# A list scheduler's prices for TensorE's small fp32 products, in one mixer instead of two

## The chip, the cores and the metric

The kernel runs on one core of a Trainium2 chip. The metric is the device time of one execution in microseconds. A profiled execution is read beside it, with the time of each instruction on TensorE (PE, and PEld for its weight loads), VectorE (DVE), ScalarE (ACT), GpSimd (POOL) and the DMA queues that SyncE (SP) and others issue.

## The reference, cut to what matters

A decoder trunk of two layers on 512 tokens of 1024 channels, in fp32. Each layer is `x <- LN(alpha*x + mixer(x))`, then `x <- LN(alpha*x + hierMoE(x))`. The first layer's mixer is RWKV-7 time mixing with causal pooling, the second's a Conformer convolution with chunkwise retention. The change reaches the second one, here in short:

```python
def conv_retention_mixer(x, w_in, conv_w, conv_b, cln_g, cln_b, gn_g, gn_b, w_out):
    p = x @ w_in
    ca, cb, q, k, v, gr = split(p)                      # 512 channels each
    u = causal_depthwise_conv(ca * sigmoid(cb), conv_w) + conv_b      # width 31
    y_conv = silu(layer_norm(u, cln_g, cln_b))
    ret = head_norm(retention(q, k, v), LN_EPS) * gn_g + gn_b
    y_ret = silu(gr) * ret
    return concatenate([y_conv, y_ret]) @ w_out
```

Retention works on 8 heads of 64 in four chunks of 128 tokens: scores `q k^T` under a decay mask, their product with `v`, a product of `q` with the state of the chunks before, and an update of that state from `k` and `v`. After the mixer the router of the expert stage takes the logits of 36 outputs for each token, from which the top group and its top two of eight experts follow.

## The kernel before, in words

`trunk_kernel` (L2228) runs `mixer0`, `moe`, `mixer1`, `moe` one behind the other. The two mixers are written as streams, Python generators that yield the engine of their next step and the tiles that it needs. `Flow` (L31) is a list scheduler that runs while the program is built: it keeps a clock of its own for every engine (`free`), when each tile is made (`made`) and last used (`used`), and in `run` (L179) it always issues the step that could start first. Where two could start at the same time (within `slack`, 0.05 us in the second mixer), the stream that stands first in the list goes first, except that `dense` goes first while the count of TensorE columns is `short` (L186 to L188). The order in which steps are issued is the order in each engine's queue; on the chip an engine works its queue in that order and waits where an operand is not there. The scheduler's clock comes from `cost` (L64), the price of an instruction by engine, operation and size, and `note` (L89) books it; `clocked` (L141) stretches a price on TensorE where it takes the engine's clock to be low, and counts columns: passes (two for fp32) times output columns times weight rows over 128.

`note` overrides the price of a TensorE product in fp32 with both weight rows and output rows at 64 or fewer: it lands in one quarter of the array, and costs its columns over 2080, or over 1040 where one of the two products before it went to the same quarter; 0.11 us is added where such products begin or end. All this is done in every `Flow`, so in both mixers. A transpose costs 0.107, any other product that is not fp32 its columns over 2330, an fp32 product its columns over 600 and at least 0.21.

The second mixer (L972) issues these streams, in the order of the list at L1440: the first weights' split (`weights`: a high half on ACT, low halves on POOL or DVE), `sums`, `turned`, the router's `ready`, `logits` and `norms` (from `start`, L1462), `join`, `ret_norm` (L1409), `retention` (L1309), `kernels`, `evacuate` (L1222), `conv_norm` (L1270), `taps` (L1145), the other `weights`, `dense` (L1173), `affine` and `turn`. What bears on the prediction:

- `dense` multiplies the input projection in steps of three products (high by high, high by low, low by high), with `x` or the weights `w` as the stationary side; in the trace `pp<-x,wh`, `pp<-x,wl`, `pp<-wh,x` and `pp<-wl,x`. Then it waits for `mc` (the convolution's result, L1190) and takes the first half of the output projection (again `pp<-wh,x`, with 512 columns), and for `mr` (the retention's, L1200) the other half (`pp<-wh,mr`).
- `conv_norm` works after the 124 taps of the convolution on DVE. For each of four blocks of 128 tokens (called the first to the fourth token below): four transposes on TensorE (`pt<-ident,acc`), statistics on DVE (`cst`, `cmv`, `crs`), a power of one column on POOL (`crs`), a scaling on DVE (`cn`), four transposes back (`pt<-ident,cn`), four Silu activations on ACT into `acc`. Then for each of four pieces a copy on ACT and a subtraction on DVE (or POOL, L1304) make the high and low halves `mc` (in the trace `x<-acc` and `x<-acc,x`).
- `retention`, per chunk: transposes of `q` and `k` (`pt<-ident,qkv`; copies `qT`, `kT` on ACT, `qx` on DVE), eight scores (`ps<-qT,kT`), a mask on DVE (`sc`), eight products with `v` (`pr<-qkv,sc`, L1361), from the second chunk on eight with the state (`pr<-R,qx`, L1368), in all but the last eight for the state's update (`ps<-qkv,kz`, L1374), then statistics and scaling on DVE with a power of eight columns on POOL (`rst`, `rmv`, `rrs`, `rn`).
- `ret_norm`: transposes of `rn`, `yr` on ACT, its product with `sgr` on DVE, and the halves `mr`.
- Banks of PSUM are handed out by name, two of each; a request waits until the last but one bank of that name has been given back (`take`, L164).

`moe` (L1562) plans its own order by `run_streams` (L218) and uses none of these prices.

Of the kernel before, what the change touches and what calls it, by code (L numbers as in the profile page):

```python
# [9 lines left out]
F32 = mybir.dt.float32  # L10
# [20 lines left out]
class Flow:  # L31
# [3 lines left out]

    HOP = {"PE": 0.2, "V": 0.13, "A": 0.2, "G": 0.13, "D": 0.0}

    def __init__(self, nc, slack=0.0, lead=1.1):
        self.nc, self.slack, self.lead = nc, slack, lead
        self.free = {e: 0.0 for e in ("PE", "V", "A", "G", "D")}  # L40
        self.made, self.used, self.rings, self.place, self.rooms, self.log = {}, {}, {}, {}, {}, []
        self.version = 0
        self.done = set()
        self.columns, self.warm = {}, {0: False}
        self.quarters = [None, None]
        self.pe, self.V, self.A, self.G, self.D = (
            Flow.Engine(self, n, e) for n, e in (("PE", nc.tensor), ("V", nc.vector), ("A", nc.scalar), ("G", nc.gpsimd),
                                                 ("D", nc.sync)))
# [14 lines left out]
    @staticmethod  # L63
    def cost(e, op, out, ins, alu=None):  # L64
        n = max(math.prod(t.shape[1:]) for t in (out, *ins))
        if e == "D":
            return math.prod(out.shape) * 4 / 355e3
        if e == "PE":
            n = math.prod(out.shape[1:])
            if op == "transpose":  # L70
                return 0.107
            if ins[0].dtype == F32:
                return max(n / 600, 0.21)
            return n / 2330
        scalars = sum(math.prod(t.shape[1:]) == 1 for t in ins) if n > 1 else 0
        if e == "V":
            if op == "reciprocal":
                return 0.066 + 0.0063 * n
            fast = op in ("tensor_scalar", "tensor_copy") and ins[0].space == bass.MemoryType.SB
            return 0.066 + 0.06 * scalars + n / (1700 if fast else 960)  # L80
        if e == "A":
            return (0.24 if len(ins) > 1 else 0.14 if scalars else 0.07) + n / 1170
        if op == "memset":
            return n / 1150
        if alu == OP.pow:
            return 0.3 + 0.165 * n
        return 0.07 + n / (445 if op == "tensor_tensor" else 1050)

    def note(self, e, op, args, kw, r):  # L89
        aps = [v for v in (*args, *kw.values()) if isinstance(v, bass.AP)]  # L90
        out, ins = (kw["out"] if "out" in kw else aps[0]), []
        for v in aps:
            if v is not out:
                ins.append(v)
        t0 = self.free["D" if op == "dma_start" else e]
        for v in ins:
            t0 = max(t0, self.at(v, e))
        k = out.tensor.name
        if k not in self.made:
            n, ring = self.enter(out.tensor)  # L100
            bufs = out.tensor.bufs or out.tensor.tag_meta.bufs
            if n >= bufs:
                t0 = max(t0, self.used.get(ring[n - bufs], 0.0) + 0.1)
        else:
            t0 = max(t0, self.used.get(k, 0.0) if not (e == "PE" and k in self.made) else 0.0)
        d = "D" if op == "dma_start" else e
        c = self.cost(d, op, out, ins, kw.get("op"))
        if e == "PE":

            here = None  # L110
            if op != "transpose" and ins[0].dtype == F32 and ins[0].shape[0] <= 64 and out.shape[0] <= 64:
                here = ins[0].start_partition, out.start_partition
                c = math.prod(out.shape[1:]) / (1040 if here in self.quarters[-2:] else 2080)
            if (here is None) != (self.quarters[-1] is None):
                c += 0.11
            self.quarters = (self.quarters + [here])[-2:]
        t1 = self.clocked(t0, c, out, ins[0], op) if e == "PE" else t0 + c
        self.free[d] = t1
        ready = t1 + (2.0 if d == "D" else 0.0)
        self.made[k] = (ready, d)  # L120
        self.used[k] = max(self.used.get(k, 0.0), ready)
        for v in ins:
            k = v.tensor.name
            self.used[k] = max(self.used.get(k, 0.0), t1)
        self.log.append((e, op, t0, t1, r, getattr(self, 'cur', '-')))
# [133 lines left out]
class Kernel:  # L259
# [39 lines left out]
    def mixer0(self):  # L299
# [2 lines left out]


        nc, tc, a = self.nc, self.tc, self.a
        flow = self.flow = Flow(nc, 0.0, 1.0)
        V, G, A, PE = flow.V, flow.G, flow.A, flow.pe
        mm = PE.matmul
        H2 = (0, 64)
# [1 line left out]
        with ctx:  # L310
# [91 lines left out]
            for t in range(NT):  # L402
                for g in range(2):
                    ps = (pp if g else pi).tile([128, 4, 128], F32, name="pp" if g else "pi")
                    for k in range(4):
                        c = 128 * (4 * g + k)
# [1852 lines left out]
```

## Time and profile before

| | us |
|---|---|
| median of three runs | 908.71 (908.58 to 909.77) |
| profiled execution, its own time | 905.55 |
| its span, first to last instruction | 903.7 |
| busy in the span: PE | 829.2 (92%) |
| PEld | 610.5 (68%) |
| DVE | 616.0 (68%) |
| ACT | 335.3 (37%) |
| POOL | 287.1 (32%) |

The page gives the busy share of every engine and TensorE's granted clock in 40 slices of the span; a view by stretch gives the same for any stretch that one names. In a timeline row, consecutive instructions of one kind are merged: start, time, engine, line, operation, tiles, count, and in brackets the idle time of the engine just before, with what ended it. Every step issued by a stream of a mixer has the line of the helper, L58, so rows are told apart by their tiles. An fp32 product is two instructions (x2) in the trace. Matmuls are pipelined, so merged rows on PE can overlap.

### The profile page before, as it was taken

What the parts mean: (1) busy time and instruction counts of PE and PEld (TensorE: products, weight loads), DVE (VectorE), ACT (ScalarE), POOL (GpSimd) and SP (SyncE); (2) the same over time, 40 slices, a digit from 0 to 9 for tenths busy, and PEclk for the clock granted to TensorE, in tenths of its full rate; (3) what the DMA queues carried; (4) which work ended last, traced back from release to release, by engine and by line L of the source; (5) the groups of instructions that cost most, each with busy time, mean ns of one, the idle gap of its engine ahead of it and who ended that gap; (6) DMA issues with size and microseconds to landing.
All of it is one profiled execution on the core that took longest, in us unless ns stands there. A gap on an engine that the chain in (4) does not pass through costs nothing. (4 is left out here: it accounts for less than half of the span.)

```text
span 903.7 us, 18556 instructions
## 1 busy us (share of the span) xinstructions
PE 829.2 (92%) x7386; PEld 610.5 (68%) x7386; DVE 616.0 (68%) x1450; ACT 335.3 (37%) x672; POOL 287.1 (32%) x302
## 2 busy tenths in 40 slices
PE   7999999899999889999968999999899787999992
PEld 5777666676777655665548889997678664546542
DVE  3586987879587776654576899985554576546457
ACT  4544243433322544444354222224313443333323
POOL 2130332334510335010048965446132018000004
PEclk9999999999999899999989999999799989999997
DMA  7210110101228699898561322323135179878932
GB/s 248 93 49 26 49 49 2 49 25 49 72 63 337 203 372 405 346 416 364 203 184 48 94 94 94 94 94 118 63 141 220 71 265 371 299 285 315 421 165 94
DMA packets 43594, 156.96 MB, mean 174 GB/s; under 512 B 4865, under 2 KB 21377, under 8 KB 35312
## 3 DMA queue, kind: packets, MB, share of 16 engines
q1 hardware_dynamic: 38128, 141.79, 41.5%
q0 software_dynamic: 4224, 9.74, 3.4%
q10 hardware_dynamic: 1152, 4.19, 1.1%
q8 instruction: 60, 0.98, 0.5%
q14 instruction: 30, 0.25, 0.1%
HBM read 154.66 MB, written 6.29 MB: 178 GB/s over the span
## 5 line engine op out<-in xcount | busy, mean ns | idle before, releaser
L58 PE MATMUL pp<-x,wh 128*128 128x512 f32 x480 | 156.9, 408 | 1.3 <-ACT wh L58 1.3
L58 PE MATMUL pp<-wh,x 128*128 128x256 f32 (+1 forms) x544 | 129.8, 326 | 3.5 <-DVE rot L58 2.8
L58 ACT CAST wh<-wr 128x512 fp32r<-128x512 f32 (+1 forms) x82 | 61.4, 776 | 146.1 <-PE pp L58 102.8
L1921 DVE SCALAR_TENSOR_TENSOR x<-x,pcm 128x512 f32<-128x512 f32 x104 | 70.7, 685 | 47.2 <-PE pcm L1919 44.6
L58 PEld LDWEIGHTS pp<-wh,x 128*128 128x128 f32 x544 | 92.8, 195 | 13.8 <-DVE x L58 3.3
L1885 PE MATMUL ph<-we,xt 128*64 128x256 f32 (+2 forms) x928 | 101.8, 383 | 0.0
L58 PEld LDWEIGHTS pp<-x,wh 128*128 128x128 f32 x480 | 84.0, 188 | 24.0 <-issue 7.0
L58 PE MATMUL pp<-x,wl 128*128 128x512 f32 x240 | 94.2, 392 | 0.5 <-DVE wl L58 0.5
L1919 PE MATMUL pcm<-yh,P 128*128 128x512 f32 x200 | 86.0, 430 | 2.7 <-DVEq L2104 1.3
L58 PE MATMUL pp<-wl,x 128*128 128x256 f32 (+1 forms) x272 | 87.0, 320 | 0.0
L1875 ACT ACTIVATE xt<-pt,x 128x128 f32<-128x128 f32 x208 | 78.7, 472 | 20.7 <-PE pt L1869 20.7
L1885 PEld LDWEIGHTS ph<-we,xt 128*64 128x64 f32 (+2 forms) x928 | 58.8, 126 | 37.0 <-issue 10.8
L58 DVE SCALAR_TENSOR_TENSOR ps<-u,cw,ps 128x512 f32<-128x512 f32 x116 | 79.5, 745 | 0.7
L1919 PE MATMUL pcm<-yl,P 128*128 128x512 f32 x200 | 79.3, 396 | 0.0
L58 POOL TENSOR_TENSOR wl<-wr,wh 128x1024 fp32r<-128x1024 f32 x28 | 67.3, 2416 | 27.1 <-ACT wh L58 27.1
L58 DVE SCALAR_TENSOR_TENSOR x<-x,pp 128x512 f32<-128x512 f32 x64 | 43.4, 684 | 34.1 <-PE pp L58 33.9
L1787 POOL DMA_INDIRECT xg<-xd,imx x20 | 19.8, 992 | 141.1 <-PE pt L1869 131.2
L1919 PEld LDWEIGHTS pcm<-yh,P 128*128 128x128 f32 x200 | 37.9, 189 | 25.9 <-DVE P L1911 9.0
L1904 PE MATMUL py<-we,hT 128*64 128x512 f32 (+2 forms) x232 | 52.4, 603 | 2.5 <-ACT hT L1895 2.5
L58 PEld LDWEIGHTS pp<-wl,x 128*128 128x128 f32 x272 | 53.0, 195 | 2.4
L58 PEld LDWEIGHTS pp<-x,wl 128*128 128x128 f32 x240 | 45.1, 188 | 10.8 <-DVE wl L58 0.9
L296 DVE TENSOR_TENSOR yl<-py,yh 128x512 fp32r<-128x512 f32 x50 | 34.4, 690 | 24.1 <-ACT yh L295 24.0
(437 smaller groups left out, 1547.6 us busy)
## 6 DMA issues: line engine op xcount, KB each, us to landing
we<-in_c_experts_dram SPq DMA_DIRECT2D x56, 1536.0 KB, 10.3
wr<-in_c_in_dram SPq DMA_DIRECT2D x18, 512.0 KB, 3.6
x<-in_c_experts_dram SPq DMA_DIRECT2D x8, 1024.0 KB, 11.3
wr<-in_od_w_in_dram SPq DMA_DIRECT2D x7, 1024.0 KB, 5.1
wr<-in_ev_w_out_dram SPq DMA_DIRECT2D x8, 512.0 KB, 3.7
x<-in_c_experts_dram SPq DMA_DIRECT2D x8, 512.0 KB, 9.3
xd<-x ACTq DMA_DIRECT2D x8, 512.0 KB, 3.9
wr<-in_od_w_in_dram SPq DMA_DIRECT2D x8, 512.0 KB, 5.8
```

The lines of the kernel that those rows point to most:

```text
L58: r = f(*args, **kw)
L296: (eng or nc.vector).tensor_tensor(lo, src, hi.bitcast(F32), op=OP.subtract)
L1787: G.indirect_dma_start(out=xg[n % NG], out_offset=None, in_=xd, in_offset=bass.IndirectOffsetOnAxis(ap=idx, axis=0), bounds_check=S - 1, o ...
L1875: A.activation(xt[:, kk], ps[:, k], AF.Identity, scale=gc[:, kk:kk + 1], bias=bc[:, kk:kk + 1])
L1885: mm(hp[r], xt[:, k, r], w[0][:, k], start=k == 0, stop=k == KT - 1)
L1904: mm(ps[r], hT[:, r], w[1][:, h], start=True, stop=True)
L1919: mm(ps, P[:, 128 * t:128 * t + 128], y[:, 512 * half:512 * half + 512], start=n == 0, stop=n == len(ops) - 1)
L1921: V.scalar_tensor_tensor(xs, xs, scale, ps, op0=OP.mult, op1=OP.add, accum_out=total)
```

## The change

`Flow` gets a flag, `quarters`, off unless it is given. `mixer0` gives it, `mixer1` does not. With the flag `note` prices TensorE's products as before. Without it `cost` alone does, and there an fp32 product with both sides at 64 rows or fewer costs 0.027 us and its columns over 1200, at least 0.08; any other fp32 product its columns over 600, at least 0.137 instead of 0.21.

```diff
--- before.py
+++ after.py
@@ -35,14 +35,14 @@
 
     HOP = {"PE": 0.2, "V": 0.13, "A": 0.2, "G": 0.13, "D": 0.0}
 
-    def __init__(self, nc, slack=0.0, lead=1.1):
+    def __init__(self, nc, slack=0.0, lead=1.1, quarters=False):
         self.nc, self.slack, self.lead = nc, slack, lead
+        self.quarters = [None, None] if quarters else None
         self.free = {e: 0.0 for e in ("PE", "V", "A", "G", "D")}
         self.made, self.used, self.rings, self.place, self.rooms, self.log = {}, {}, {}, {}, {}, []
         self.version = 0
         self.done = set()
         self.columns, self.warm = {}, {0: False}
-        self.quarters = [None, None]
         self.pe, self.V, self.A, self.G, self.D = (
             Flow.Engine(self, n, e) for n, e in (("PE", nc.tensor), ("V", nc.vector), ("A", nc.scalar), ("G", nc.gpsimd),
                                                  ("D", nc.sync)))
@@ -70,7 +70,8 @@
             if op == "transpose":
                 return 0.107
             if ins[0].dtype == F32:
-                return max(n / 600, 0.21)
+                narrow = ins[0].shape[0] <= 64 and out.shape[0] <= 64
+                return max(0.027 + n / 1200, 0.08) if narrow else max(n / 600, 0.137)
             return n / 2330
         scalars = sum(math.prod(t.shape[1:]) == 1 for t in ins) if n > 1 else 0
         if e == "V":
@@ -105,12 +106,14 @@
             t0 = max(t0, self.used.get(k, 0.0) if not (e == "PE" and k in self.made) else 0.0)
         d = "D" if op == "dma_start" else e
         c = self.cost(d, op, out, ins, kw.get("op"))
-        if e == "PE":
-
-            here = None
-            if op != "transpose" and ins[0].dtype == F32 and ins[0].shape[0] <= 64 and out.shape[0] <= 64:
-                here = ins[0].start_partition, out.start_partition
-                c = math.prod(out.shape[1:]) / (1040 if here in self.quarters[-2:] else 2080)
+        if e == "PE" and self.quarters:
+
+            here, n = None, math.prod(out.shape[1:])
+            if op != "transpose" and ins[0].dtype == F32:
+                c = max(n / 600, 0.21)
+                if ins[0].shape[0] <= 64 and out.shape[0] <= 64:
+                    here = ins[0].start_partition, out.start_partition
+                    c = n / (1040 if here in self.quarters[-2:] else 2080)
             if (here is None) != (self.quarters[-1] is None):
                 c += 0.11
             self.quarters = (self.quarters + [here])[-2:]
@@ -302,7 +305,7 @@
 
 
         nc, tc, a = self.nc, self.tc, self.a
-        flow = self.flow = Flow(nc, 0.0, 1.0)
+        flow = self.flow = Flow(nc, 0.0, 1.0, quarters=True)
         V, G, A, PE = flow.V, flow.G, flow.A, flow.pe
         mm = PE.matmul
         H2 = (0, 64)
```

## Rows read from the trace of the kernel before

**Rows 1.** Busy time by stretch: from us to us, length, then each engine, granted clock, DMA.

```profile
642.10:712.00 69.90, 68.75 (x396) 57.16 (x396) 32.48 (x92) 17.19 (x27) 15.99 (x13) 0.93 0.33 133
```

**Rows 2.** The same view: the stretch before the output products, and the one after it.

```profile
629.30:642.10 12.80, 6.98 (x49) 6.00 (x48) 7.58 (x11) 10.73 (x23) 5.34 (x3) 0.85 0.42 155
...
642.10:649.10 7.00, 7.00 (x43) 5.04 (x42) 0.81 (x2) 0.17 (x1) 0.00 (x0) 0.55 0.02 7
```

**Rows 3.** Groups by form, TensorE, 600 to 720 us: count | busy us, mean ns | idle before.

```profile
L58 PE MATMUL pr<-qkv,sc 128*128 128x64 f32 x64 | 9.4, 310 | 3.8 <-DVE sc L58 3.8
...
L58 PE MATMUL ps<-x,x 128*128 128x36 f32 x64 | 7.6, 272 | 0.0
...
L58 PE MATMUL pr<-R,qx 64*128 64x64 f32 x48 | 4.2, 327 | 0.0
...
L58 PE MATMUL ps<-qkv,kz 128*64 128x64 f32 x48 | 2.1, 228 | 0.0
```

**Rows 4.** Timeline, TensorE: the first product whose price changes.

```profile
604.06 1.89 PE L58 MATMUL pr<-qkv,sc 128*128 128x64 f32 x16
```

**Rows 5.** Timeline, TensorE: between the third token's two sets of transposes.

```profile
617.32 0.60 PE L58 MATMUL pt<-ident,acc 128*128 128x128 f32 x4
...
617.76 1.90 PE L58 MATMUL pr<-qkv,sc 128*128 128x64 f32 x16
...
620.33 1.11 PE L58 MATMUL pr<-R,qx 64*128 64x64 f32 x16
...
621.37 0.73 PE L58 MATMUL pp<-x,wh 128*128 128x512 f32 x2
...
622.26 0.69 PE L58 MATMUL ps<-qkv,kz 128*64 128x64 f32 x16
...
623.68 0.60 PE L58 MATMUL pt<-ident,cn 128*128 128x128 f32 x4
```

**Rows 6.** Timeline, DVE: conv_norm, qx, yr, the last subtraction, and rn beside POOL.

```profile
619.79 0.81 DVE L58 TENSOR_SCALAR cn<-pt,cmv,crs 128x512 f32<-128x512 f32 x1 [0.73 <-POOL crs L58]
...
630.72 0.69 DVE L58 TENSOR_TENSOR qx<-pt,xz 128x512 f32<-128x512 f32 x1 [0.93 <-ACT qT L58]
...
635.96 1.53 DVE L58 TENSOR_TENSOR yr<-yr,sgr 128x512 f32<-128x512 f32 x1 [1.66 <-ACT yr L58]
...
641.53 0.68 DVE L58 TENSOR_TENSOR x<-acc,x 128x512 fp32r<-128x512 f32 x1
...
665.64 2.88 DVE L58 TENSOR_TENSOR rn<-rn,rrs 128x512 f32<-128x512 f32 x1 [0.57 <-POOL rrs L58]
```

**Rows 7.** Timeline, ACT: the weight cast, the fourth Silu, the first yr.

```profile
629.15 1.05 ACT L58 CAST wh<-wr 128x1024 fp32r<-128x1024 f32 x1 [3.33 <-POOL crs L58]
...
631.07 1.51 ACT L58 ACTIVATE acc<-pt,vec 128x128 f32<-128x128 f32 x4
...
634.37 1.56 ACT L58 ACTIVATE yr<-pt,vec 128x128 f32<-128x128 f32 x4
```

**Rows 8.** Timeline, TensorE: the third chunk and the first output product.

```profile
638.74 3.67 PE L58 MATMUL pr<-qkv,sc 128*128 128x64 f32 x16 [3.78 <-DVE sc L58]
...
642.18 0.77 PE L58 MATMUL pp<-wh,x 128*128 128x512 f32 x1
...
643.74 1.97 PE L58 MATMUL pr<-R,qx 64*128 64x64 f32 x16
...
648.50 0.68 PE L58 MATMUL ps<-qkv,kz 128*64 128x64 f32 x16
```

**Rows 9.** Timeline, POOL: the second token's power, and low halves of weights.

```profile
611.71 0.93 POOL L58 TENSOR_TENSOR crs<-crs,nhalf 128x1 f32<-128x1 f32 x1 [1.14 <-DVE crs L58]
...
612.61 2.39 POOL L58 TENSOR_TENSOR wl<-wr,wh 128x1024 fp32r<-128x1024 f32 x1
...
634.59 2.35 POOL L58 TENSOR_TENSOR wl<-wr,wh 128x1024 fp32r<-128x1024 f32 x1 [1.97 <-ACT wh L58]
...
665.58 5.20 POOL L58 TENSOR_TENSOR wl<-wr,wh 128x1024 fp32r<-128x1024 f32 x2
```

## The prediction, made before the change was run

> **What bounds the kernel now.** I read the stretches first. From 642.10 to 712.00 us, the rest of the second mixer, TensorE is busy 68.75 of 69.90 us [rows 1]: there the time is TensorE's work, whatever its order. From 712.00 on the second expert stage runs; it has a planner of its own that the diff does not touch, so what the mixer gains or loses is handed on to the end. The exception is the stretch just ahead: from 629.30 to 642.10 TensorE is busy 6.98 of 12.80 us, and in the 7.00 us after it the granted clock averages 0.55, that is nearly all at 1.2 and not 2.4 GHz [rows 2]. Call this the hole. The dense products of the input projection have run out there, and those of the output projection wait for all four pieces of `mc`, the result of `conv_norm`. So the chain of `conv_norm`, four tokens one behind the other (the Silu writes the `acc` tiles that the next token's transposes read), sets when the hole ends, and TensorE's work outside it sets the rest.
>
> **What changes.** In the first mixer nothing: its flow sets `quarters`, and the branch in `note` then gives every F32 product the price it has now. In the second mixer no product has both sides at 64 rows or fewer (scores write 128 rows, the `kz` products have 128-row weights), so the two-quarter prices never held there. What is left is the floor of a wide F32 product, 0.21 before and 0.137 after; it bites below 126 columns. That is 128 products: 32 `pr<-qkv,sc`, 24 `pr<-R,qx`, 24 `ps<-qkv,kz`, 32 of the router and 16 of its constants; each is two instructions in the trace, hence x64, x48, x48 and x64 [rows 3]. Scores keep 128/600 = 0.213. No instruction is added, removed or changed, no DMA either (SP's loads follow the steps that free their buffers); only the order written into each engine's queue can move, and only behind the first product with a new price. That is the `pr` batch at 604.06 [rows 4]: all before it keeps its order, and so its cost is nothing.
>
> **How the prices stand to the chip.** In the third token's stretch eight `pr` take 1.90 us, eight `R,qx` 1.11, eight `kz` 0.69 [rows 5], together 3.70. The scheduler now books 24 x 0.21 = 5.04, afterwards 24 x 0.137 = 3.29. The new sum is nearer (0.41 short against 1.34 over), though `pr` alone is then booked at 1.10 for 1.90.
>
> **Term A, the third token.** Between its two sets of transposes (617.32 and 623.68) stand three retention batches, each followed by a dense step of three products [rows 5]. The dense steps get there because the scheduler counts TensorE columns against its own clock and takes `dense` first when they run short. A product with 128-row weights earns 128 columns; at 0.21 that is 609 per planned us, at 0.137 it is 934, and the need of the `short` test lies between. So I expect two of the three dense steps to slip behind the `cn` transposes: 622.26 - 621.37 = 0.89 and, from the end of `kz`, 623.68 - 622.95 = 0.73, together 1.6 us earlier. `cn` itself is ready at 619.79 + 0.81 = 620.60 [rows 6], so TensorE's queue is the limit, and the saving is real.
>
> **Term B, the fourth token.** With cheaper products the next chunk's retention is planned sooner, and I expect the transposes of its keys to be queued ahead of the fourth `cn` transposes. They wait for `qx` (0.69 us on DVE, behind `cn`) [rows 6], and ACT's weight cast (1.05) falls ahead of the Silu [rows 7]. 0.69 + 1.05 = 1.74 gives term A back. I book A + B at zero: the fourth Silu ends at 631.07 + 1.51 = 632.58 as now.
>
> **Term C, from there to the output products.** Now 642.18 - 632.58 = 9.6 us: ACT alternates the four `acc` copies with a cast and two `yr` activations, and DVE's last subtraction starts at 641.53 [rows 6 to 8]. If retention of the third chunk is queued earlier, its masked scores leave this queue, and the second `yr` falls behind the copies. What stays is a cast 1.05, one `yr` 1.56, DVE's product 1.53, then four subtractions at 0.68 ahead of the last, and 0.65 from the last's start to the first product: 632.58 + 1.05 + 1.56 + 1.53 + 2.72 + 0.65 = 640.09. That is 2.1 us gained; the ends are 0 (order as now) and 9.6 less the four subtractions and 0.65, some 6.
>
> **Term D, what moves into the hole.** `pr` of the third chunk starts at 638.74, having waited 3.78 for `sc`; `R,qx` (1.97 us at the low clock) and `kz` (0.68) follow only after the hole, between dense products [rows 8]. With `sc` earlier they run while TensorE has nothing else. As the low clock lasts its time anyway, I count them at the full-clock rows, 1.11 + 0.69 = 1.8 (ends: 0 and 1.97 + 0.68 = 2.65).
>
> **A price that may come on top.** DVE's product of `yr` takes 1.53 us where a subtraction with both inputs in SBUF takes 0.68, and `rn` at 665.64 takes 2.88 [rows 6], each beside POOL's low halves of a weight, from 634.59 and from 665.58 [rows 9]. The Trainium skill (SBUF — State Buffer, Who interferes with whom) says that a DVE instruction with two SBUF inputs and a GpSimd one that reads SBUF exclude each other for the whole instruction; these rows agree. By that rule term C would be no gain wherever POOL's halves lie over the four subtractions, and it is a rival below. In the sum I keep the one hit that the rows of now show.
>
> **Sum.** A + B 0, C -2.1, D -1.8: -3.9 us. The profiled execution took 905.55 us (span 903.7), so it would be 901.65; the median of the runs is 908.71, 3.16 above it, and I carry the same difference over: 904.8.
>
> **The rivals.**
> Given back at the shared port: the four subtractions meet both POOL halves. A hit costs 2.88 - 0.68 = 2.20; two cost 4.40, of which `yr` pays 0.85 now, so 3.55 comes back and 908.4 is left. For it: both halves of the next weights are due in this very stretch. Against: of the four subtractions of now at least the last runs at its bare 0.68.
> Slower: a POOL half ahead of a power. At the second token `crs` runs on POOL at 611.71 and a half of `wl`, 2.39 us, directly after it at 612.61 [rows 9]. If the new order books that half first, `cn` waits 2.39 longer, all later tokens with it, and no dense work is left to cover that: 908.7 + 2.4 = 911.1 (913.5 if it happens at two tokens). It decides at the point where the half's cast is booked as done before DVE's small statistics; their lead now is 0.90. For it: a shift of 16 x 0.073 = 1.2 booked us in the first chunk alone is more than that lead. Against: most of that shift moves both.
> Faster: the hole closes. Idle 12.80 - 6.98 = 5.82 and 7.00 x 0.45 = 3.15 of low clock: 9.0 less, 899.7. Against: the chain of four tokens has waits on ACT, DVE and POOL that no price on TensorE removes.
> Nothing moves: no pick flips and the order is the same, 908.7. Against: 0.073 us exceeds the scheduler's slack of 0.05 at every product.
>
> **Chances.** Forecast 0.50 (its own range 902.5 to 906.9), port 0.20, nothing 0.03, slower 0.17, hole closes 0.10. A measurement of this kernel can tell about 0.2% (1.8 us) from no change. Faster 0.50 + 0.10 = 0.60, same 0.20 + 0.03 = 0.23, slower 0.17. The range 901.0 to 911.2 leaves out the closed hole and the upper half of the slower case, under 0.2.
>
> **What would show it.** Right: the queue identical up to 604; 617 to 624 with one dense step between the third token's transposes, not three; `R,qx` and `kz` of the third chunk before the first output product; that product some 2 us earlier against the start of `pr` at 604; from there the same 68 us of TensorE less 1.8. Port: DVE subtractions of 2 us or more in the hole beside POOL's `wl`. Slower: `cn` of the second or third token waiting on `crs` with a `wl` ahead of it. I am wrong if the hole is as long as now and `R,qx` still lies behind it, or if an idle stretch of TensorE opens elsewhere after 604, at the router above all.

## The result, and the profile after

The changed kernel takes 899.64 us (median of 13 runs, 893.85 to 904.48), the kernel before 906.17 in the same comparison (median of 13, 903.29 to 911.19). The ratio is 0.9918, 95% interval 0.9896 to 0.9939: 7.4 us less (5.5 to 9.4), about twice the forecast 3.9, and 899.64 lies below the lower end of the forecast range, 901.0. Single runs of both kernels spread over 8 to 11 us, so only ratios with intervals are used below. The profiled execution took 899.8 us, its span is 897.7, and its engines did what they did before:

```profile
PE 829.0 (92%) x7386; PEld 611.0 (68%) x7386; DVE 613.9 (68%) x1450; ACT 336.6 (37%) x672; POOL 286.7 (32%) x302
```

The first `pr` batch, up to which the order of every queue is the same as before, starts at 606.29 instead of 604.06: the stages ahead of it vary by that much between two profiles. So positions are given **from each profile's own first `pr` batch**; from there to the end of the span it was 903.7 - 604.06 = 299.64 us and is 897.7 - 606.29 = 291.41, 8.23 less. Such a length varies too: in e1 and e2 below, whose runs are as long as those before, it is 298.05 and 297.27, and in e2 2.1 of the 2.4 us of difference lie behind the mixer's router.

The timeline of TensorE after the change, to be laid beside [rows 4, 5 and 8]:

```profile
606.29 1.89 PE L58 MATMUL pr<-qkv,sc 128*128 128x64 f32 x16
...
619.54 0.60 PE L58 MATMUL pt<-ident,acc 128*128 128x128 f32 x4
619.98 1.90 PE L58 MATMUL pr<-qkv,sc 128*128 128x64 f32 x16
621.81 1.11 PE L58 MATMUL pr<-R,qx 64*128 64x64 f32 x16
622.85 0.73 PE L58 MATMUL pp<-x,wh 128*128 128x512 f32 x2
...
623.74 0.69 PE L58 MATMUL ps<-qkv,kz 128*64 128x64 f32 x16
624.35 0.66 PE L58 MATMUL pt<-ident,cn 128*128 128x128 f32 x4
...
632.86 1.16 PE L58 MATMUL ps<-qT,kT 64*128 64x128 f32 x16 [0.56 <-ACT kT L58]
...
634.80 2.00 PE L58 MATMUL pr<-qkv,sc 128*128 128x64 f32 x16 [0.19 <-DVE sc L58]
636.73 1.11 PE L58 MATMUL pr<-R,qx 64*128 64x64 f32 x16
...
638.35 0.69 PE L58 MATMUL ps<-qkv,kz 128*64 128x64 f32 x16
638.97 0.50 PE L58 MATMUL pp<-wh,x 128*128 128x512 f32 x1
...
647.45 0.50 PE L58 MATMUL pp<-wh,x 128*128 128x512 f32 x1 [1.45 <-DVE x L58]
```

Three things are to be seen. One dense step stands between the third token's two sets of transposes, not three. `pr` of the third chunk waits 0.19 us for `sc`, not 3.78, and runs in 2.00 us, not 3.67. And the hole [rows 2] is gone: `R,qx` and `kz` run ahead of the first output product.

DVE tells why. First TensorE's scores before; then DVE's timeline before, around the `yr` product of [rows 6]; then DVE's after:

```profile
633.22 1.16 PE L58 MATMUL ps<-qT,kT 64*128 64x128 f32 x16
```

```profile
633.60 0.69 DVE L58 TENSOR_TENSOR x<-acc,x 128x512 fp32r<-128x512 f32 x1 [2.20 <-ACT x L58]
...
637.41 0.68 DVE L58 TENSOR_TENSOR x<-acc,x 128x512 fp32r<-128x512 f32 x1
638.01 0.68 DVE L58 TENSOR_TENSOR sc<-ps,dm 128x512 f32<-128x512 f32 x1
```

```profile
634.05 1.29 DVE L58 TENSOR_TENSOR sc<-ps,dm 128x512 f32<-128x512 f32 x2 [2.60 <-PE ps L58]
635.26 0.68 DVE L58 TENSOR_TENSOR x<-acc,x 128x512 fp32r<-128x512 f32 x1
637.61 1.53 DVE L58 TENSOR_TENSOR yr<-yr,sgr 128x512 f32<-128x512 f32 x1 [1.67 <-ACT yr L58]
639.06 0.68 DVE L58 TENSOR_TENSOR x<-acc,x 128x512 fp32r<-128x512 f32 x1
...
640.44 1.29 DVE L58 TENSOR_TENSOR x<-acc,x 128x512 fp32r<-128x512 f32 x2
```

Before, the eight scores that `sc` masks began at 633.22 and took 1.16, so `sc` could have started at 634.4. But it stood in DVE's queue behind the `yr` product, for which DVE waited 1.66 us until 635.96, and behind a subtraction, and started at 638.01. After, both `sc` stand ahead of all that and start as the scores come.

The idle time and the clock follow. Busy time by stretch (from us to us, length, then PE, PEld, DVE, ACT, POOL busy, granted clock, DMA share, GB/s), two slices before and then three after:

```profile
604.00:642.10 38.10, 32.28 (x248) 27.03 (x247) 23.73 (x75) 19.37 (x41) 17.58 (x12) 0.95 0.30 106
...
640.00:650.00 10.00, 10.00 (x57) 7.90 (x57) 3.24 (x8) 2.02 (x5) 0.00 (x0) 0.58 0.23 91
```

```profile
604.00:642.10 38.10, 37.27 (x317) 31.52 (x317) 24.26 (x75) 19.14 (x41) 17.79 (x12) 1.00 0.29 100
...
640.00:650.00 10.00, 8.47 (x50) 6.13 (x49) 8.91 (x33) 4.05 (x9) 1.65 (x1) 1.00 0.37 141
...
670.00:680.00 10.00, 9.19 (x35) 7.78 (x35) 1.33 (x4) 0.46 (x1) 5.29 (x3) 0.66 0.88 365
```

In the first stretch TensorE idles 38.10 - 37.27 = 0.83 us, where it idled 5.82. Where 0.58 was granted in 640 to 650, it is now 1.00. A new wait of 1.45 us stands in that slice (the row at 647.45: TensorE waits for an accumulation into `x`, behind the third chunk's statistics on DVE), and a low clock at the router in 670 to 680 (0.66; before, 0.96 there and 0.87 in the next ten).

The router's batch before, and then after:

```profile
674.75 1.87 PE L58 MATMUL ps<-x 128*128 128x36 f32 x16
```

```profile
668.22 1.87 PE L58 MATMUL ps<-x 128*128 128x36 f32 x16
```

The 8.23 us, place by place, from the first `pr` batch: the first output product stood at 642.18 - 604.06 = 38.12 and stands at 638.97 - 606.29 = 32.68, **5.44 earlier**, of which 3.67 - 2.00 = 1.67 is `pr` at the higher clock; the router's `ps<-x` batch at 674.75 - 604.06 = 70.69 and now 668.22 - 606.29 = 61.93, 8.76 earlier, so **3.32 more** in between. Behind the router 0.5 is given back, less than two profiles differ by there.

### The profile page after: what moved, and what is told of

Read it like the earlier page. It is cut to its first block, busy times and chain, and to the rows that moved or that the text cites. A ratio compares the mean times of both kernels' runs of the same rounds, so it can differ in the third digit from the quotient of the medians.

```text
span 897.7 us, 18553 instructions
## 1 busy us (share of the span) xinstructions
PE 829.0 (92%) x7386; PEld 611.0 (68%) x7386; DVE 613.9 (68%) x1450; ACT 336.6 (37%) x672; POOL 286.7 (32%) x302
```

## The experiments

**What was to be told apart.** The theory: the gain is the queue place of the third chunk's `sc` in DVE's queue, which ends TensorE's wait and with it the drop of the clock. Its rivals: the router's new price, the earlier third token (term A), the moved work (term D), or simply prices nearer to the truth. All ratios are to the kernel before, timed beside each; they come from 12 runs of the kernel (6 of e3 and of e5, 13 of the change). This table is worked out from the timelines, as above; the last two columns are the granted clock in 640 to 650 and the ratio with its interval. That slice is fixed while the first `pr` batch starts between 604.06 and 610.10, so in e1, e7 and e11 the low clock reaches into the next ten us (0.89, 0.81 and 0.69). Where `pr` is cut in two (e8, e9), its first half is given.

| kernel | third `pr` | first output product | clock | ratio |
|---|---|---|---|---|
| before | +34.68 | +38.12 | 0.58 | 1 |
| after | +28.51 | +32.68 | 1.00 | 0.9918 (0.9896 to 0.9939) |
| e1 router only | +34.68 | +38.12 | 0.60 | 0.9989 (0.9970 to 1.0008) |
| e2 retention first | +34.69 | +38.12 | 0.54 | 1.0008 (0.9986 to 1.0030) |
| e3 first two chunks | +28.51 | +31.89 | 1.00 | 0.9904 (0.9881 to 0.9927) |
| e4 filler of 16 | +37.65 | +39.35 | 1.00 | 1.0003 (0.9977 to 1.0028) |
| e5 scores booked as measured | +31.10 | +34.51 | 1.00 | 0.9885 (0.9854 to 0.9915) |
| e6 filler of 8 | +34.69 | +36.80 | 1.00 | 0.9949 (0.9926 to 0.9973) |
| e7 last two chunks | +34.68 | +40.19 | 0.68 | 0.9980 (0.9950 to 1.0011) |
| e8 measured prices | +31.51 | +35.71 | 0.64 | 0.9974 (0.9950 to 0.9997) |
| e9 masks behind `yr` | +33.49 | +40.80 | 0.56 | 0.9989 (0.9962 to 1.0017) |
| e10 change and scores | +28.49 | +32.48 | 0.83 | 0.9947 (0.9922 to 0.9973) |
| e11 first two and scores | +28.49 | +32.66 | 0.83 | 0.9943 (0.9911 to 0.9975) |
| e12 last two and scores | +31.10 | +34.06 | 1.00 | 0.9928 (0.9901 to 0.9955) |

**e1: the new price for the router's products alone.** In the changed kernel's `cost`:

```diff
-                return max(0.027 + n / 1200, 0.08) if narrow else max(n / 600, 0.137)
+                return max(0.027 + n / 1200, 0.08) if narrow else max(n / 600, 0.137 if n == 36 else 0.21)
```

> The new price (0.137) for the router's 48 products alone; retention's 80 keep 0.21. Theory (the gain is made in the hole between 628 and 650 us): the order up to the router is that of the kernel before, so no change, within 0.25% (2 us) of it; the hole is as long as before, first output product some 38 us after the first pr batch, low clock behind it. Rival (the gain comes from the order of router and output products after 670 us): 2 us or more faster.

Nothing to be measured: the hole stands as before (wait 3.78). The router's part of the change is worth 1.0 us by the middle of the interval, 2.7 at most, and that is not clear of zero.

**e2: the old prices, `retention` ahead of `ret_norm` in the list of streams**, meant to put `sc` ahead of `yr`:

```diff
-            flow.run([weights(0, 1), sums(), turned(), *begin, *(join(t) for t in range(NT)), ret_norm(), retention(), kernels(), evacuate(), conv_norm(), taps((0, 2)), taps((1, 3)), weights(1), dense(), affine(), *(turn(h, g) for h in range(2) for g in range(4))])
+            flow.run([weights(0, 1), sums(), turned(), *begin, *(join(t) for t in range(NT)), retention(), ret_norm(), kernels(), evacuate(), conv_norm(), taps((0, 2)), taps((1, 3)), weights(1), dense(), affine(), *(turn(h, g) for h in range(2) for g in range(4))])
```

> Old prices; only the list of streams is changed, retention stands ahead of ret_norm, so that a tie on DVE goes to retention's mask sc of the third chunk. Theory (TensorE stands still in the hole because its pr batch waits 3.78 us for sc, which stands in DVE's queue behind ret_norm's work): pr starts 2 to 4 us earlier, the output products follow, 2.5 to 6 us faster, though the third token keeps its three dense steps. Rival 1 (the third token's dense steps, term A): no change, within 2 us. Rival 2 (the last of the four subtractions ends the hole, term C): no change or slower, since the subtractions do not come sooner.

A miss: the edit did not reach its state. The timelines of DVE and then TensorE:

```profile
637.03 1.53 DVE L58 TENSOR_TENSOR yr<-yr,sgr 128x512 f32<-128x512 f32 x1 [1.66 <-ACT yr L58]
638.48 0.68 DVE L58 TENSOR_TENSOR x<-acc,x 128x512 fp32r<-128x512 f32 x1
639.09 1.28 DVE L58 TENSOR_TENSOR sc<-ps,dm 128x512 f32<-128x512 f32 x2
```

```profile
639.82 3.68 PE L58 MATMUL pr<-qkv,sc 128*128 128x64 f32 x16 [4.37 <-DVE sc L58]
```

The list's order decides only between steps that could start at the same time, and `sc` was not planned for the time of `yr` at all. The scheduler's own plan, its log of times while the program is built, shows why: it books the third chunk's eight scores at 3.41 us (0.427 each, that is 0.213 doubled, since it takes TensorE's clock as low there), where the trace has 1.16; so on its clock the first `yr` product stands at 171.45 and the first `sc` at 172.75. The changed prices let it book the same scores at 0.213 each and 5 us sooner, `sc` at 165.32 and `yr` at 168.02. What the new prices do here is done by way of that.

**e3: the new floor for the retention products of the first two chunks only**, and **e7: of the last two only.** The old prices, and in `retention` the `pr`, `R,qx` and `kz` products through:

```diff
+                def cmm(*args, **kw):
+                    flow.cheap = n < 2          # e7: n >= 2
+                    mm(*args, **kw)
+                    flow.cheap = False
...
-        if e == "PE":
+        if e == "PE" and getattr(self, "cheap", False):
+            c = max(math.prod(out.shape[1:]) / 600, 0.137)
+        elif e == "PE":
```

> The new price for retention's products of the first two chunks only (40 products); the last two chunks and the router keep 0.21. The queues are those of the changed kernel up to the third chunk's kz batch, and differ behind it (third and fourth chunk's later work, router). Theory (all of the gain lies up to the end of the hole): 6 to 8 us faster, as the full change. Rival (the gain is made by the order behind the hole, fourth chunk and router): at most 2 us faster.

> The new price for retention's products of the last two chunks only. Up to the third chunk's pr batch the queues are those of the kernel before, sc behind yr included; R,qx then follows pr directly, ahead of the output products, and kz comes sooner between them. Theory: nothing is gained where TensorE still waits for sc; between 1 us faster and 0.5 us slower. Rival (term D: state products moved ahead of the output products are worth 1.8 us by themselves): 1.5 to 3 us faster.

e3 has the whole gain, with `pr` at +28.51 as after. In e7 `R,qx` moves up to right behind `pr`, but `pr` waits 3.78 us for `sc` as before, and both run at the low clock:

```profile
644.06 3.67 PE L58 MATMUL pr<-qkv,sc 128*128 128x64 f32 x16 [3.78 <-DVE sc L58]
647.67 1.97 PE L58 MATMUL pr<-R,qx 64*128 64x64 f32 x16
649.57 0.79 PE L58 MATMUL pp<-wh,x 128*128 128x512 f32 x1
```

So the moved work alone (term D) gives nothing that is clear of zero: 1.8 us less by the middle of the interval, which reaches from 4.5 less to 1.0 more, and 0.7 less up to the router by the profile. That interval does not rule out the 1.8 us of term D; but it is no substitute for the gain, and what matters is settled by prices ahead of the third chunk.

**e4 and e6: how much of it is the clock?** The kernel before, with 16 (e4) or 8 (e6) extra products put into the hole, ahead of the third chunk's `pr`, which then starts its sums anew:

```diff
+                        if n == 2 and not g:
+                            idle = prs[0].rearrange("p a b -> p (a b)")
+                            for _ in range(16):         # e6: 8
+                                nc.tensor.matmul(idle, self.ident, dm[:, :2].rearrange("p a b -> p (a b)"), start=True, stop=True)
```

> The kernel before with 16 products of 256 columns added (identity times a mask table, 3.4 us of TensorE at full clock) just ahead of the third chunk's pr batch, into the bank that this batch then overwrites; the result is unchanged, the order of all else too. They fill the 3.78 us for which TensorE waits for sc. Theory (the low clock behind the hole is a large part of the gain): granted clock 1.0 through 642 to 649, pr batch 1.9 instead of 3.67, 3.5 to 5 us faster in spite of more work. Rival (only the idle time counts, the clock does not): no change or slower by up to 1 us.

> As e4, with 8 filler products instead of 16: in e4 the sixteen took 7.07 us, not 3.4, and pr started 3 us later for it. Eight take 3.5 us and end before sc is there. Theory (low clock is a large part): pr starts where it did and takes 1.9, granted clock 1.0 behind it, 3.5 to 5 us faster. Rival (the clock does not count for the end): within 1.5 us of the kernel before.

e4 was mis-sized: its filler took 7.07 us, double of what I had put in, and `pr` started 3 us later; the clock stayed up, and the two cancel (1.0003). e6 has it right. TensorE's timeline:

```profile
638.09 3.62 PE L1362 MATMUL pr<-dm,ident 128*128 128x256 f32 x16
642.04 2.31 PE L58 MATMUL pr<-qkv,sc 128*128 128x64 f32 x16 [0.33 <-DVE sc L58]
```

```profile
640.00:650.00 10.00, 9.57 (x73) 7.50 (x73) 7.39 (x20) 3.77 (x8) 0.24 (x1) 1.00 0.39 142
```

`pr` starts where it did (+34.69), every queue keeps its order, TensorE does 3.62 us more work, and the kernel is 0.51% faster, 4.6 us (2.4 to 6.7). The only thing that it takes away is the low clock: 0.58 becomes 1.00 in 640 to 650, and at the router, where before had 0.96 and 0.87, 1.00 is granted too. By its profile nearly all of this is made in the first place: `pr` takes 2.31 instead of 3.67, the first output product comes 1.32 earlier, and the router's batch 4.11 (+66.58 for +70.69). The changed kernel keeps the clock up there too, though not at the router (0.66). So about 4 of its 8.76 us up to the router are the clock, an estimate from single profiles; the rest is the idle time that went, less the new wait.

**e5: the old prices, and only the third chunk's scores booked at what the trace has.**

```diff
+                    t0 = max(flow.free["PE"], flow.at(qT, "PE"), flow.at(kT, "PE"))
                     for i in range(4):
...
+                    if n == 2:
+                        flow.free["PE"] = t0 + 1.16
+                        for ps, _ in pss:
+                            flow.made[ps.tensor.name] = t0 + 1.16, "PE"
+                            flow.used[ps.tensor.name] = t0 + 1.16
```

> All prices old; only the third chunk's eight scores are booked at the 1.16 us that the trace shows, where the scheduler books 3.41 (0.213 each, doubled since it takes the clock to be low). The order is that of the kernel before up to these scores; behind them the two masks sc come ahead of yr and the second subtraction in DVE's queue, and pr and R,qx ahead of the output products in TensorE's. Theory (the queue of DVE in the hole, sc behind yr, is the cause): pr starts 3 us earlier or more, the clock stays up, 5 to 7.5 us faster. Rival (the third and fourth token's order, terms A and B, is needed): at most 2 us faster.

No price differs from before, the third token has its three dense steps as before, and the whole gain is there (0.9885, 10.4 us; 7.7 to 13.2), more than I had expected. DVE, then TensorE:

```profile
634.98 1.29 DVE L58 TENSOR_TENSOR sc<-ps,dm 128x512 f32<-128x512 f32 x2
636.53 1.54 DVE L58 TENSOR_TENSOR yr<-yr,sgr 128x512 f32<-128x512 f32 x1 [0.26 <-ACT yr L58]
```

```profile
635.73 2.00 PE L58 MATMUL pr<-qkv,sc 128*128 128x64 f32 x16 [0.78 <-DVE sc L58]
```

Both `sc` are ahead of `yr`, and TensorE waits 0.78. Terms A and B are not needed for the gain.

**e9: the reversal.** The changed kernel, with the third chunk's masks made to queue behind the first `yr` product:

```diff
+                    if n == 2:
+                        yield from wait(("yr", 0))
...
+                    done.add(("yr", n))
```

> The changed kernel with one condition added: the third chunk's masks sc are issued only when the first yr product has been, so that they stand behind it in DVE's queue, as before the change. The order on TensorE up to pr and the prices are those of the change. Theory (that queue place is the cause): pr starts some 33 us after the first pr batch instead of 28.5, TensorE stands still for it and the clock falls; 0 to 3 us faster than the kernel before, most of the gain is gone. Rival (the gain comes from the third and fourth token and the moved batches): 6 us or more faster, as the change.

The gain is gone (0.9989). DVE, TensorE and the stretch:

```profile
635.78 1.53 DVE L58 TENSOR_TENSOR yr<-yr,sgr 128x512 f32<-128x512 f32 x1 [1.66 <-ACT yr L58]
637.24 1.27 DVE L58 TENSOR_TENSOR sc<-ps,dm 128x512 f32<-128x512 f32 x2
```

```profile
637.97 1.97 PE L58 MATMUL pr<-qkv,sc 128*128 128x64 f32 x8 [5.17 <-DVE sc L58]
...
642.33 1.97 PE L58 MATMUL pr<-R,qx 64*128 64x64 f32 x16
...
645.28 0.80 PE L58 MATMUL pp<-wh,x 128*128 128x512 f32 x1
```

```profile
640.00:650.00 10.00, 10.00 (x57) 8.69 (x56) 5.49 (x27) 2.63 (x6) 2.93 (x2) 0.56 0.23 88
```

All new prices are in force, the third token runs as in the changed kernel, `R,qx` and `kz` still stand ahead of the first output product, and with the one queue place undone the wait (5.17), the low clock (0.56) and the old time are back. With e5 this is shown from both sides: the queue place is the cause. In both runs the scheduler's later steps follow the place, so what is shown is the place together with what it brings on.

**e8: prices as the trace has them** (`pr` and router 0.237, products of 64 weight rows 0.137, `kz` 0.086):

```diff
-                return max(0.027 + n / 1200, 0.08) if narrow else max(n / 600, 0.137)
+                rows, wide = ins[0].shape[0], math.prod(ins[0].shape[1:])
+                return max(0.027 + n / 1200, 0.08) if narrow else 0.137 if rows == 64 and n <= 128 else 0.086 if wide == 64 else max(n / 600, 0.237)
```

> Each small product of the second mixer at the price that the trace of before shows: pr and router 0.237, R,qx and scores 0.137 to 0.145, kz 0.086. Rival (nearer prices make the better order): as fast as the changed kernel or faster, 7 to 10 us below the kernel before. Theory (the gain hangs on one queue place, sc against yr on DVE, and on no price as such): pr waits less only as far as sc moves; one sc moves ahead of yr here, so 2 to 6 us faster, less than the changed kernel.

Better prices are not what helps: 0.26% (0.03 to 0.50), against 0.82 (0.61 to 1.04). Only one of the two `sc` comes ahead of `yr`, `pr` is cut in two, and TensorE runs at the low clock already when it starts; the eight scores ahead of it took 1.70 us, not 1.16:

```profile
634.86 0.69 DVE L58 TENSOR_TENSOR sc<-ps,dm 128x512 f32<-128x512 f32 x1 [0.64 <-PE ps L58]
635.88 1.54 DVE L58 TENSOR_TENSOR yr<-yr,sgr 128x512 f32<-128x512 f32 x1 [0.33 <-ACT yr L58]
637.34 0.68 DVE L58 TENSOR_TENSOR sc<-ps,dm 128x512 f32<-128x512 f32 x1
```

```profile
635.60 1.97 PE L58 MATMUL pr<-qkv,sc 128*128 128x64 f32 x8 [0.77 <-DVE sc L58]
```

Its waits up to there (0.3, 1.3, 0.5 and 0.8 us in the view of waits) sum up to what e5 has (0.6, 0.9, 0.5 and 0.8), and yet the clock fell in e8, ahead of `pr`'s wait, and not in e5. Why stays open.

**e10 to e12: e5's edit on top of the change, of e3 and of e7.**

> The changed kernel with the third chunk's scores booked at 1.16 us as in e5. The place of sc is already the good one, so both effects are one: between 7 and 11 us faster than the kernel before, not the sum of the two. Rival (they add): 15 us or more.

> e3 with the third chunk's scores booked at 1.16 us: as e3 and e5, 8 to 11 us faster than the kernel before.

> e7 with the third chunk's scores booked at 1.16 us. Theory: the order of e7 behind pr with the masks at their good place, so 8 to 11 us faster than the kernel before where e7 alone was within its noise. Rival (e5's gain hung on the order of the later batches): at most 4 us faster.

e12 lifts e7 from 0.9980 to 0.9928 (the intervals just touch): the queue place again (`pr` now waits 0.78), less than e5 alone by the middle of the intervals. e10 and e11 are no better than the change, and e10's interval lies wholly behind e5's: the gains don't add up, and at 4.8 and 5.2 us both are below what I had expected. Their rows show what may eat it. In e10, DVE, then POOL, then TensorE:

```profile
636.28 1.85 DVE L58 TENSOR_TENSOR yr<-yr,sgr 128x512 f32<-128x512 f32 x1 [2.25 <-ACT yr L58]
638.05 2.85 DVE L58 TENSOR_TENSOR x<-acc,x 128x512 fp32r<-128x512 f32 x1
```

```profile
633.97 1.29 POOL L58 TENSOR_TENSOR x<-acc,x 128x512 fp32r<-128x512 f32 x1 [4.26 <-ACT x L58]
635.22 5.14 POOL L58 TENSOR_TENSOR wl<-wr,wh 128x1024 fp32r<-128x1024 f32 x2
```

```profile
640.96 0.73 PE L58 MATMUL pp<-wh,x 128*128 128x512 f32 x2 [2.08 <-DVE x L58]
```

The scheduler gave the first subtraction to POOL (L1304 chooses), both `wl` halves follow back to back, and DVE's first subtraction, the second of the four, takes 2.85 us beside them where it takes 0.68 otherwise; TensorE waits 2.08 for it, and the clock in 640 to 650 is 0.83. e11 has the same rows (2.86 and 1.86). This is read from the rows; no run put the subtraction back alone.

The lowest ratio is that of e5 (896.43 us, six runs), the old prices with one booking corrected; its interval overlaps that of e3 and of the change, so that it is better than these is not shown.

## Why the prediction was right or wrong

**Right.** The direction. The order of the queues: the same up to the first `pr` batch, one dense step for three at the third token, `R,qx` and `kz` ahead of the first output product. Term A: the third token's `cn` transposes stood at 623.68 - 604.06 = 19.62 and stand at 624.35 - 606.29 = 18.06, 1.56 earlier against the 1.6 predicted. A and B together: the fourth Silu ends at 632.58 - 604.06 = 28.52 before and at 633.20 + 1.52 - 606.29 = 28.43 after (the row below), zero as booked.

```profile
633.20 1.52 ACT L58 ACTIVATE acc<-pt,vec 128x128 f32<-128x128 f32 x4
```

That zero is in part luck: the cast that term B adds stood ahead of this Silu before too (629.15 in [rows 7]). What took term A back is that the fourth `cn` is ready 1.17 earlier, its transposes start 0.46 earlier, behind two more dense steps and the key transposes, and the Silu starts 0.10 earlier, behind one more copy (`kT`, 0.58) on ACT. That `sc` of the third chunk would move was foreseen as well, in terms C and D; what failed is what that is worth.

**Wrong: what ends the hole.** "So the chain of `conv_norm` ... sets when the hole ends" is the step that failed. After the change the first output product starts at 638.97, ahead of the last two subtractions at 640.44: the output products take the pieces of `mc` one by one as they come, and don't wait for the last. What held them was the queue: `pr` of the third chunk stands ahead of them on TensorE, `pr` waited 3.78 us for `sc`, and `sc` waited on DVE behind `yr`. The row with that wait was in [rows 8], and DVE's wait for `yr` in [rows 6]; I used the first for term D only. Term C was put at 2.1 for the wrong reason; the first output product came 5.44 earlier with the moved `R,qx` and `kz` already run, which term D had counted apart.

**Wrong: the clock.** "As the low clock lasts its time anyway" is the second step. With the wait gone the clock does not fall there: its price was in the prediction (7.00 us at 0.55, that is 3.15), but only in the rival of the closed hole, and without the 1.67 that `pr` itself lost to it. e6, with the clock up there and at the router, gains 4.6 (2.4 to 6.7), by its middle more than the whole forecast of 3.9.

**The sum, as measured.** A and B -0.1; from the fourth Silu to the first output product -5.35 (with the moved work run, and 1.67 of it `pr` at the higher clock; C was -2.1); then 1.8 of moved work less and 3.15 of low clock less, against 1.45 of new wait: -3.5 (-3.32 by the rows); +0.5 behind the router, within what profiles differ by. Together some -8.3, by the profile; -7.4 by the runs. The error is C, too small by 3.25, and the 3.15 of low clock, left out, against a new wait of 1.45 that nothing in the sum stood for.

**The rivals.** The closed hole, at a chance of 0.10, is nearly what happened: 9.0 us stated, 5.5 to 9.4 measured, idle time of 5.82 down to 0.83. Against it I had said that no price on TensorE removes a wait on DVE; the prices did remove one, by moving `sc` in DVE's queue. That its 899.7 meets the measured 899.64 is in part luck, since the median of before was 906.17 here and not 908.71. The rival of the shared port did not strike the subtractions of the changed kernel (0.68 for one; `yr` at 1.53 as before), but rows as it foresaw stand in e10 and e11, 2.85 and 2.86 for 0.68 beside POOL's `wl`. A POOL half ahead of a power did not come: the fourth `cn` waited 0.44 us for `crs`, with no `wl` ahead of it. Of the signs I had named for being wrong, an idle stretch opening elsewhere, a small one did: 1.45 us at 647.45. The low clock at the router came as well; no run ties the two.

**Open.** Why the clock at the router's 36-column products is 0.66 in 670 to 680 after the change, 0.83 in e5 and 1.00 in e4 and e6; and why it fell in e8.

## What to carry to other kernels

Where an engine works its queue in order, look for the instruction at the head of the queue in each idle stretch, and then for what stands ahead of its operand on the other engine: here 3.78 us of waiting came from one mask queued behind a product that was not ready. The scheduler's prices mattered here where they flipped such a place, so find the place and correct the booking that causes it (e5), rather than all prices (e8). And count an idle stretch of TensorE together with a low clock behind it: here the clock was about half of the gain up to the router (about 4 of 8.76 us, estimated from e6's profile).

## What the runs showed that was not expected

An fp32 product of 256 columns with 128 weight rows took 3.62 / 8 = 0.45 us in e6 at a granted clock of 1.00, two instructions of 0.23, where a `pr` product of 64 columns takes 1.90 / 8 = 0.24: four times the columns for twice the time. And more work made the kernel faster: e6 adds 3.62 us to TensorE and saves 4.6 (2.4 to 6.7).
